# Hybrid decoder trunk on one core: bias table as eight DRAM rows, and one convolution group moved from TensorE to GpSimd

## The chip, the core and the metric

The kernel runs on one NeuronCore of a Trainium2 chip. The metric is the device time of one execution in microseconds (us). Before the change it is 2148.73 us, the median of three runs (2148.67 to 2150.67). Five engines work side by side and meet at semaphores: TensorE (PE; its weight loads are shown as PEld), VectorE (DVE), ScalarE (ACT), GpSimd (POOL) and SyncE (SP), which here only issues DMAs.

## What is computed

One layer of a hybrid decoder over 2064 prompt positions and 8 sample positions. Cut to what matters:

```python
q, k, v, u = project_in(x, norm1_g, w_in)            # rmsnorm, h @ w_in, u = a * sigmoid(b)
s = einsum(q, k) * HEAD_DIM ** -0.5
bias = rel_bias[t5_bucket(clip(dist, 0, WINDOW))]    # table over distance 0..128, one row per head
s = where(valid, s + bias, -inf)                     # then softmax with sinks, and p @ v
c = depthwise_conv(pad(u, 30), conv_w, conv_b)       # causal, 31 taps, 512 channels
c = silu(layernorm(c, conv_ln_g, conv_ln_b))
x = x + concat(attn, c) @ w_out
x = x + relu(rmsnorm(x) @ w_up) ** 2 @ w_down
```

For a query at row p of a block and a key at column j, the bias depends on p - j alone: row p of the table of one head is the row before it shifted by one place.

## The kernel before

Channels lie on the 128 partitions, positions in the free dimension. The positions are cut into five tiles (384, 448, 448, 448 and 320 prompt positions). Every large product is made in three float32r passes: weights and activations are split into a high and a low part, and hi*hi, hi*lo and lo*hi are added in PSUM. One step (`pe_step`) is one slab of 128 output channels: 8 chunks in 3 passes, 24 matmuls, in the order hi, lo of chunk 0, hi, lo of chunk 1 and so on with the weights' high part, then the eight with their low part. ACT and DVE split the next slab meanwhile (`whi`, `wlo`).

Tile 0 goes first. Its input projection has 14 steps: m = 8 to 13 (keys, values, queries), then m = 0 and 1 alone, then m = 2 to 7, each paired with the same slab for tile 1. The steps m = 2c and 2c + 1 give the gate and the values of convolution group c (128 channels), so group 0 is ready after m = 1 and group 3 after m = 7. Then five more steps of tile 1 serve as cover, and the output projection of tile 0 (`wout_step`) reads the attention output (`cah`, `cal`) and the convolution output. From there on the feed-forward part of one tile covers the small work of the next.

Small work comes from generators (`Background`): attention (`attn_gen`), convolution and its layer norm (`conv_gen`), norms. Each step hands out a budget of it in the order of the generators' list, and `sync_bg` writes out what is left. The tile framework then orders every engine's instructions by its own timeline of the program. So the order on an engine isn't the order in the code, and each engine runs its list strictly in order.

Tiles that live long come from `slot()`: one pool of 52 buffers for inputs, normalised chunks, queries, convolution accumulators and scratch. A buffer is handed out again as soon as the program text is done with it, and the first instruction that writes it then waits for the last one that read the tile before it.

The bias: `bias_setup` makes the 8 rows of 384 distances with a small matmul, writes them to DRAM 128 times (`scr`, 1.5 MB, once per partition) and reads them back with a stride one element short of a row, so that each partition gets its shifted row (`bias`). It is called at the sixth input step of tile 0 (BAT = 5). The first score operation of the attention (L562, DVE) needs `bias`.

The convolution of tile 0: DVE runs groups 0 to 2, 31 operations each (one multiply, then 30 multiply-adds over shifted views of u, L122 and L116) into the accumulators `pre[c]`; `conv_pe_gen` runs group 3 on TensorE as 31 matmuls with diagonal weights that ACT builds (`cps`). `misc()` is a single PSUM buffer called `st` that many small products share.

Of the kernel before, what the change touches and what calls it, by code (L numbers as in the profile page):

```python
# [7 lines left out]
F32 = mybir.dt.float32  # L8
F32R = mybir.dt.float32r
AF = mybir.ActivationFunctionType  # L10
ALU = mybir.AluOpType
# [5 lines left out]
NSMP = 8  # L17
HD = 64
NH = 8
WIN = 128  # L20
CW = 31
# [13 lines left out]
EW = 384  # L35
# [3 lines left out]
G1, G2, GF, CWT, CB, LG, LB, SK, SKR = 0, 8, 16, 24, 148, 152, 156, 160, 168  # L39
# [3 lines left out]
STEP = "step"  # L43
# [33 lines left out]
def trunk(tc, x_in, w_all, smalls, rel, ck, cv, sconv, y_out, kv_out, ck_out, cv_out, up_out, us_out):  # L77
    nc = tc.nc
    with ExitStack() as ctx:
# [4 lines left out]
        at = ctx.enter_context(tc.tile_pool(name="at", bufs=1))  # L84
        dr = ctx.enter_context(tc.tile_pool(name="dr", bufs=1, space=bass.MemoryType.DRAM))
# [4 lines left out]
        def ahead(gen, off, cond=None):  # L90
            while True:
                try:
                    if off and (cond is None or cond()):
                        with tc.high_priority(off):
                            r = next(gen)
                    else:
                        r = next(gen)
                except StopIteration:
                    return
                yield r  # L100
# [28 lines left out]
        def act(out, a, f, bias=0.0, scale=1.0, accum_out=None):  # L129
            if accum_out is None:  # L130
                return nc.scalar.activation(out, a, f, bias=bias, scale=scale)  # L131
            return nc.scalar.activation(out, a, f, bias=bias, scale=scale, accum_out=accum_out)  # L132
# [7 lines left out]
        def slot(dt=F32):  # L140
            t = tp.tile([128, TS], dt, tag="t", name="t")
            return t
# [12 lines left out]
        def mm(out, lhsT, rhs, start, stop):  # L155
            return nc.tensor.matmul(out, lhsT, rhs, start=start, stop=stop)  # L156
# [11 lines left out]
        sq0 = cp.tile([128, 1], F32, name="sq0")  # L168
        act(sq0, epst, AF.Sqrt)
        bias = cp.tile([128, NH, 256], F32, name="bias")  # L170
        scr = dr.tile([128, NH, EW], F32, name="scr")

        order = []
        pos = {"dma": 0, "split": 0}
# [532 lines left out]
        def conv_gen(i):  # L707
# [4 lines left out]
            cvs = s["cvs"] = {}  # L712
            pre = [slot() for _ in range(4)] if i == 0 else None
            s["pre"] = pre
            todo = [c for c in range(4) if i > 0 or c not in CPE]
            groups = [todo[j:j + CG] for j in range(0, len(todo), CG)]

            def taps(c, a):
# [102 lines left out]
                tt(s["cvl"][c][:, :r], cvs[c][:, :r], f(s["cvh"][c][:, :r]), ALU.subtract)  # L821
                yield

        def conv_pe_gen(i):
            s = st[i]
            n = RT[i]
            o = OFF[i]
            while "cvs" not in s:
                yield STEP
            dgs = [slot(), slot()]  # L830
            for c in CPE:
                while c not in s.get("udone", []):
                    yield STEP
                u = s["u"][c]
                ps = pm.tile([128, 512], F32, tag="mm", name="cps")
                for k in range(CW):
                    j = CWT + c * CW + k
                    dg = dgs[k // 3 % 2][:, k % 3 * 128:k % 3 * 128 + 128]
                    act(dg, idn, AF.Copy, scale=sm[:, j:j + 1])
                    mm(ps[:, :n], dg, u[:, o + k:o + k + n], k == 0, k == CW - 1)  # L840
                    if k % PEK == PEK - 1:
                        yield STEP
                yield STEP
                a = s["pre"][c]
                act(a[:, :n], ps[:, :n], AF.Identity, bias=sm[:, CB + c:CB + c + 1])
                s["cvs"][c] = a
                yield STEP

# [74 lines left out]
        def bias_setup():  # L923
            ps = misc()
            mm(ps[:NH, :EW], relt[:33, 0:NH], relt[:33, 8:8 + EW], True, True)
            e = slot()
            cpy(e[:NH, :EW], ps[:NH, :EW])
            nc.gpsimd.dma_start(scr.rearrange("p h x -> h p x"),
                                e[:NH, :EW].unsqueeze(1).broadcast_to([NH, 128, EW]))
            a = scr[:]  # L930
            nc.gpsimd.dma_start(bias, bass.AP(tensor=a.tensor, offset=a.offset + 127,
                                              ap=[[NH * EW - 1, 128], [EW, NH], [1, 256]]))

        def ff_budget(i, up):
            t = 24 * (RT[i] / 2400.0 + 0.0025)
# [77 lines left out]
        for op in prog:  # L1013
            k = op[0]
            if k == "in":
                _, i, m = op
                if i == 0:
                    if nin == N1AT:
                        gens["n1"] = [bg.add(g1)]
                    if nin == BAT:  # L1020
                        bias_setup()
                    nin += 1
                win_step(i, m, 24 * (TI[i] / 2400.0) - 1.2 - 0.6)
            elif k == "in2":
                m = op[1]
                win_step(0, m, 24 * (TI[0] / 2400.0) - 1.2 - 0.6, keep=True)
                win_step(1, m, 24 * (TI[1] / 2400.0) - 0.6)
            elif k == "conv0":
                flush()
                gens["conv"] = [bg.add(ahead(conv_gen(0), HP0, lambda: "ln" in st[0])), bg.add(conv_pe_gen(0), True)]  # L1030
            elif k == "attn0":
                flush()
                gens["attn"] = [bg.add(attn_gen(0, range(j, PT[0] // BQ[0], NS0)), A0F) for j in reversed(range(NS0))]
            elif k == "out":
                _, i, m = op
                wout_step(i, m, ff_budget(i, False))
            elif k == "ff":
                _, i, t, g, c = op
                b = ff_budget(i, t == "u")
                if t == "u":  # L1040
                    up_step(i, g * 8 + c, b)
                else:
                    down_step(i, g, c, b)
            elif k == "bg":
                i = op[1]
                flush()
                cat_alloc(i)
                gens["attn"] = [bg.add(attn_gen(i, range(j, PT[i] // BQ[i], NS1))) for j in range(NS1)]
                if i == NT - 1:
                    gens["attn"].append(bg.add(sample_gen(i)))  # L1050
                gens["conv"] = [bg.add(ahead(conv_gen(i), HPC, lambda: "ln" in st[i]))]
            elif k == "sync_bg":
                flush()
                bg.drain(gens["attn"] + gens["conv"])
            elif k == "n1":
                gens["n1"] = [bg.add(norm1_gen(op[1]))]
            elif k == "sync_n1":
                bg.drain(gens["n1"])
            elif k == "n2":
                gens["n2"] = [bg.add(ahead(norm2_gen(op[1]), HPN if op[1] else HPN0))]  # L1060
            elif k == "sync_n2":
                flush()
                bg.drain(gens["n2"])
            elif k == "fin":
                gens["fin"] = [bg.add(ahead(final_gen(op[1]), HPF if op[1] == NT - 1 else 0))]
                if op[1] == NT - 1:
                    flush()
                    bg.drain()
# [16 lines left out]
HPN0 = 300  # L1085
HPF = 0
COV = 5
BAT = 5
N1AT = 3
A0F = False  # L1090
QUICK = ["a0", "a1", "l0", "m0", "b0", "f4"]
NS0 = 2
NS1 = 1
NPB = 2
PEK = 16
CG = 1
PARTS1 = 4
CPE = [3]


def _pack(inp):
# [107 lines left out]
```

## Time and profile before

| | us |
|---|---|
| median of three runs | 2148.73 |
| the profiled execution | 2149.5 |
| its span in the trace | 2147.7 |
| PE busy in the span | 2093.9 (97%) |
| DVE busy in the span | 1524.6 (71%) |
| ACT busy in the span | 1178.0 (55%) |
| POOL busy in the span | 50.2 (2%) |

The profiled execution lies 0.8 us over the median and 1.8 us over its own span. Busy shares are means over the whole span. For a change in one place, read the stretch it lies in: which engine stands idle there, and what ended its idle time. The chain of waits, followed back from the last instruction, tells which engine the end hangs on; the timeline of an engine in a window tells when it stood still and for whom.

### The profile page before, as it was taken

The page shows a single profiled execution, that of the slowest core. Times are in us where ns is not written, and L with a number is a line of the kernel's source. Part 1 is how long each engine was busy: PE and PEld are TensorE (multiplying, and loading weights), DVE is VectorE, ACT ScalarE, POOL GpSimd, SP SyncE. Part 2 cuts the span into 40 slices and gives each one's busy share as a digit, 9 for nine tenths or more (in the row PEclk, how much of TensorE's full clock was granted, in tenths as well). Part 3 has the DMA queues.
Part 4 walks back from the last instruction along what each step waited for, and adds up shares of the span by engine and source line. Part 5 has one row for each costly group of instructions (what it writes and reads, how often), then busy time and mean ns, then how long its engine had stood idle before and what let it go on. Part 6 is the DMA issues. An engine that isn't in the chain of part 4 may idle for free.

```text
span 2147.7 us, 29970 instructions
## 1 busy us (share of the span) xinstructions
PE 2093.9 (97%) x11330; PEld 1963.9 (91%) x11330; DVE 1524.6 (71%) x2595; ACT 1178.0 (55%) x2152; POOL 50.2 (2%) x95
## 2 busy tenths in 40 slices
PE   8599999999999999999999999999999999999998
PEld 7587999999999999999999999999999999999997
DVE  5597598986867988647759887466898754575444
ACT  6357475567546464655445547554655475454443
POOL 1000000000000000000000000000010100000000
PEclk9799999999999999999999999999999999999999
DMA  5411423334443222325432322344433323434443
GB/s 180 79 50 40 138 90 127 118 118 142 156 140 102 98 98 106 101 98 177 139 104 99 105 99 90 107 142 169 144 116 106 124 99 103 151 139 169 148 147 104
DMA packets 77952, 255.67 MB, mean 119 GB/s; under 512 B 9805, under 2 KB 20173, under 8 KB 77808
## 3 DMA queue, kind: packets, MB, share of 16 engines
q1 hardware_dynamic: 72000, 238.08, 32.3%
q0 software_dynamic: 5088, 14.93, 2.5%
q8 instruction: 89, 1.46, 0.3%
q10 hardware_dynamic: 720, 0.76, 0.1%
q14 instruction: 55, 0.45, 0.1%
HBM read 241.97 MB, written 11.75 MB: 118 GB/s over the span
## 4 chain that ended last, share of the span: by engine, by line
PE 94%; issue 2%; DMA 2%; DVE 1%; POOL 0%; ACT 0%; DVEq 0%; POOLq 0%; ACTq 0%
PE mm L156 88%; PE st L156 2%; DMA scr<-t 2%; PE s L156 1%; PE pt L581 1%; PE cps L156 1%; DVE t L116 0%; DMA bias<-scr 0%; DMA t<-x_in 0%; DVE t L112 0%; DVE wlo L112 0%; DVE m L116 0%; PE mx L156 0%; DVE ss L112 0%; PE st L529 0%
## 5 line engine op out<-in xcount | busy, mean ns | idle before, releaser
L156 PE MATMUL mm<-t,whi 128*128 128x448 f32 (+3 forms) x6560 | 1353.2, 352 | 12.8 <-ACT t L131 8.6
L156 PEld LDWEIGHTS mm<-t,whi 128*128 128x128 f32 x6560 | 1170.1, 189 | 84.1 <-ACT t L131 9.5
L135 ACT CAST whi<-raw 128x1024 fp32r<-128x1024 f32 x424 | 443.6, 1049 | 572.8 <-PE mm L156 463.1
L156 PE MATMUL mm<-t,wlo 128*128 128x448 f32 (+3 forms) x3280 | 713.5, 350 | 0.0
L112 DVE TENSOR_TENSOR wlo<-raw,whi 128x1024 fp32r<-128x1024 f32 x424 | 516.8, 1219 | 244.1 <-PE mm L156 125.3
L156 PEld LDWEIGHTS mm<-t,wlo 128*128 128x128 f32 x3280 | 588.8, 188 | 33.6
L116 DVE SCALAR_TENSOR_TENSOR t<-u,sm,t 128x448 f32<-128x448 f32 (+1 forms) x480 | 300.9, 645 | 3.5
L112 DVE TENSOR_TENSOR t<-mm,t 128x448 f32<-128x448 f32 (+2 forms) x200 | 116.6, 583 | 191.5 <-PE mm L156 190.2
L112 DVE TENSOR_TENSOR t<-m,t 128x448 fp32r<-128x448 f32 (+3 forms) x236 | 134.2, 582 | 25.9 <-ACT t L135 25.4
L135 ACT CAST t<-m 128x448 fp32r<-128x448 f32 (+3 forms) x236 | 125.3, 536 | 17.8 <-DVE m L116 13.2
L131 ACT ACTIVATE m<-mm 128x448 f32<-128x448 f32 (+2 forms) x176 | 90.1, 512 | 55.9 <-PE mm L156 50.0
L131 ACT ACTIVATE m<-t 128x448 f32<-128x448 f32 (+3 forms) x140 | 72.0, 543 | 62.1 <-DVE t L112 42.2
L132 ACT ACTIVATE p<-p,nm 112x240 f32<-112x240 f32 (+3 forms) x152 | 72.2, 476 | 50.3 <-DVE nm L121 50.1
L131 ACT ACTIVATE m<-m 128x448 f32<-128x448 f32 (+3 forms) x164 | 90.1, 549 | 3.9
L562 DVE CUSTOM_DVE_ANT_0 p<-s,bias,sm 112x240 f32<-112x240 f32 (+3 forms) x152 | 61.2, 449 | 28.0 <-DMA bias<-scr 25.6
L131 ACT ACTIVATE p<-p,rd 112x240 f32<-112x240 f32 (+3 forms) x152 | 61.9, 476 | 4.7 <-DVE rd L127 4.2
L112 DVE TENSOR_TENSOR ss<-ss,m 128x448 f32<-128x448 f32 (+3 forms) x100 | 58.4, 584 | 6.8 <-ACT m L131 3.3
L116 DVE SCALAR_TENSOR_TENSOR t<-t,sm 128x384 f32<-128x384 f32 (+1 forms) x98 | 57.2, 613 | 2.4 <-ACT t L131 1.9
L127 DVE RECIPROCAL rs<-m 128x448 f32<-128x448 f32 (+2 forms) x15 | 41.6, 2776 | 24.1 <-ACT m L131 24.1
L156 PE MATMUL mm<-cah,whi 128*128 128x448 f32 (+2 forms) x160 | 56.2, 353 | 0.0
L156 PE MATMUL mm<-cal,whi 128*128 128x448 f32 (+2 forms) x160 | 56.0, 352 | 0.0
L920 POOL DMA_DIRECT2D y_out<-t x32 | 17.3, 544 | 1609.6 <-DVE t L116 1607.7
(174 smaller groups left out, 1139.3 us busy)
## 6 DMA issues: line engine op xcount, KB each, us to landing
raw<-w_all SPq DMA_DIRECT2D x424, 512.0 KB, 3.2
t<-x_in SPq DMA_DIRECT2D x40, 224.0 KB, 4.5
y_out<-t POOLq DMA_DIRECT2D x24, 224.0 KB, 3.3
t<-x_in SPq DMA_DIRECT2D x16, 164.0 KB, 3.7
t<-x_in POOLq DMA_DIRECT2D x8, 224.0 KB, 6.5
t<-x_in SPq DMA_DIRECT2D x8, 200.0 KB, 4.7
scr<-t POOLq DMA_DIRECT2D x1, 1536.0 KB, 33.1
t<-x_in SPq DMA_DIRECT2D x8, 192.0 KB, 4.3
```

The costliest lines, as they stand in the source:

```text
L112: return nc.vector.tensor_tensor(out, a, b, op=op)
L116: return nc.vector.scalar_tensor_tensor(out, a, s, b, op0=op0, op1=op1)
L127: return nc.vector.reciprocal(out, a)
L131: return nc.scalar.activation(out, a, f, bias=bias, scale=scale)
L132: return nc.scalar.activation(out, a, f, bias=bias, scale=scale, accum_out=accum_out)
L135: return nc.scalar.copy(out, a)
L156: return nc.tensor.matmul(out, lhsT, rhs, start=start, stop=stop)
L562: nc.vector.tensor_tensor_reduce(out=p[:bq, c, :nk], in0=sp[c // 2][:bq, c % 2, :nk], in1=bias[:bq, h, b0:b0 + nk], scale=1.0, scalar=sm[: ...
L581: nc.tensor.transpose(t[:r, c * bq:(c + 1) * bq], p[:bq, c, a:a + r], idn[:bq, :bq])
L920: q.dma_start(y_out[:, YO[i] + c * n:YO[i] + (c + 1) * n], y[:, :n])
```

## The change

Two edits. First, the bias: `scr` shrinks to 8 copies of the rows (NSMP, which the sample attention still reads), and `bias_setup` moves from the sixth input step to the second (BAT = 1). Two DMAs read overlapping rows from it, so that partition p gets the row shifted by p (`brow`, in the two buffers of the attention's `p`). The shift runs the wrong way round, and four matmuls with an exchange matrix (`flip`, made on POOL) turn the partitions round, each into `st`, from which ACT copies two heads into `bias`. That is called three input steps later. Second, in tile 0 the convolution group on TensorE is dropped; group 0 goes to POOL instead (31 multiplies and 30 adds, with two product buffers), and DVE runs groups 1 to 3.

```diff
-        scr = dr.tile([128, NH, EW], F32, name="scr")
+        scr = dr.tile([NSMP, NH, EW], F32, name="scr")
...
-            todo = [c for c in range(4) if i > 0 or c not in CPE]
+            todo = [c for c in range(4) if i > 0 or c not in CPOOL]
...
-        def conv_pe_gen(i):
+        def conv_pool_gen(i):
...
-            dgs = [slot(), slot()]
-            for c in CPE:
+            prods = [slot(), slot()]
+            for c in CPOOL:
...
-                ps = pm.tile([128, 512], F32, tag="mm", name="cps")
-                for k in range(CW):
-                    j = CWT + c * CW + k
-                    dg = dgs[k // 3 % 2][:, k % 3 * 128:k % 3 * 128 + 128]
-                    act(dg, idn, AF.Copy, scale=sm[:, j:j + 1])
-                    mm(ps[:, :n], dg, u[:, o + k:o + k + n], k == 0, k == CW - 1)
...
-                act(a[:, :n], ps[:, :n], AF.Identity, bias=sm[:, CB + c:CB + c + 1])
+                wc = CWT + c * CW
+                nc.gpsimd.tensor_scalar(a[:, :n], u[:, o:o + n], sm[:, wc:wc + 1], sm[:, CB + c:CB + c + 1],
+                                        op0=ALU.mult, op1=ALU.add)
+                for k in range(1, CW):
+                    p = prods[k % 2]
+                    nc.gpsimd.tensor_scalar(p[:, :n], u[:, o + k:o + k + n], sm[:, wc + k:wc + k + 1], None,
+                                            op0=ALU.mult)
+                    nc.gpsimd.tensor_tensor(a[:, :n], a[:, :n], p[:, :n], op=ALU.add)
...
-                                e[:NH, :EW].unsqueeze(1).broadcast_to([NH, 128, EW]))
+                                e[:NH, :EW].unsqueeze(1).broadcast_to([NH, NSMP, EW]))
             a = scr[:]
-            nc.gpsimd.dma_start(bias, bass.AP(tensor=a.tensor, offset=a.offset + 127,
-                                              ap=[[NH * EW - 1, 128], [EW, NH], [1, 256]]))
+            flip = slot()
+            nc.gpsimd.memset(flip[:, :128], 0.0)
+            nc.gpsimd.affine_select(out=flip[:, :128], in_=flip[:, :128], compare_op=ALU.not_equal, fill=1.0,
+                                    base=-127, pattern=[[1, 128]], channel_multiplier=1)
+            rows = []
+            for j in range(2):
+                t = at.tile([128, 4, 256], F32, tag="p", name="brow", bufs=NPB)
+                nc.gpsimd.dma_start(t, bass.AP(tensor=a.tensor, offset=a.offset + 4 * j * EW,
+                                               ap=[[1, 128], [EW, 4], [1, 256]]))
+                rows.append(t)
+            return flip, rows
+
+        def bias_flip(flip, rows):
+            for h in range(0, NH, 2):
+                ps = misc()
+                mm(ps, flip[:, :128], rows[h // 4][:, h % 4:h % 4 + 2, :], True, True)
+                cpy(bias[:, h:h + 2, :], ps.rearrange("p (h j) -> p h j", h=2))
...
-                        bias_setup()
+                        rows = bias_setup()
+                    if nin == BAT + 3:
+                        bias_flip(*rows)
...
-BAT = 5
+BAT = 1
...
-CPE = [3]
+CPOOL = [0]
```

The framework orders the whole of tile 0 anew. The first place is TensorE after the third step of the queries. `s` are scores, `st` the single buffer, `st<-relt` the eight bias rows, `st<-brow` the flips. Before:

```order
L156 MATMUL mm<-t,whi 128x400 x10
L156 MATMUL mm<-t,wlo 128x400 x8
L156 MATMUL s<-t 128x256 x4
L156 MATMUL st<-m,ones 128x128 x3
L156 MATMUL st<-m,ones 128x64
L156 MATMUL st<-relt 8x384
L156 MATMUL mm<-t,whi 128x400 x16
```

After:

```order
L156 MATMUL mm<-t,wlo 128x400 x3
L156 MATMUL s<-t 128x256 x2
L156 MATMUL st<-brow,t 128x512 x4
L156 MATMUL st<-m,ones 128x128 x3
L156 MATMUL st<-m,ones 128x64
L529 MATMUL st<-idn,t 128x128
L530 MATMUL st<-idn,t 128x128
L156 MATMUL mm<-t,whi 128x400 x16
```

The bias rows' matmul has moved four steps up, and four flips stand in a row in front of the norm's broadcast of tile 1.

The second place is DVE at the start of the convolution of group 1. `t<-m 128x400` is u of a group of tile 0, `L122 ... t<-t,sm` the first operation of a group, `L116 ... t<-t,sm` the others. Before:

```order
L112 TENSOR_TENSOR m<-mm,t 128x400
L116 SCALAR_TENSOR_TENSOR t<-t,sm 128x384
L112 TENSOR_TENSOR t<-m 128x400
L116 SCALAR_TENSOR_TENSOR t<-t,sm 128x384
L122 TENSOR_SCALAR t<-t,sm 128x384
L116 SCALAR_TENSOR_TENSOR t<-t,sm 128x384
```

After, u of group 1 stands 44 rows ahead of these, and u of group 2 another 22 rows behind that:

```order
L112 TENSOR_TENSOR wlo<-raw,whi 128x1024
L112 TENSOR_TENSOR dn<-dn,es 128x4
L122 TENSOR_SCALAR t<-t,sm 128x384 x2
L127 RECIPROCAL rd<-dn 128x4
L112 TENSOR_TENSOR p<-st,p 64x4x128
L116 SCALAR_TENSOR_TENSOR t<-t,sm 128x384 x4
```

Groups 1 and 2 now begin together, well behind their u. In the built program their accumulators take the buffers of two low-part chunks of tile 0's normalised input, and the second product buffer of POOL takes a third; all three wait for matmuls 2, 4 and 6 of step m = 7, the last that reads those chunks. Before, group 0 and 1 had buffers that were free, and group 2 alone waited for m = 7.

The third place is DVE at the end of the convolution. Here `m<-t` and `m<-m,t` add the four groups for the layer norm. Before:

```order
L127 RECIPROCAL rd<-dn 128x4
L112 TENSOR_TENSOR vv<-st,vv 128x128
L112 TENSOR_TENSOR m<-m,t 128x384 x2
L112 TENSOR_TENSOR wlo<-raw,whi 128x1024
L112 TENSOR_TENSOR kk<-mm,kk 64x448 x2
L112 TENSOR_TENSOR p<-st,p 64x4x128
L116 SCALAR_TENSOR_TENSOR t<-mx,t 128x384 x4
```

After:

```order
L112 TENSOR_TENSOR p<-st,p 64x4x128
L116 SCALAR_TENSOR_TENSOR t<-t,sm 128x384 x4
L112 TENSOR_TENSOR cal<-p,cah 64x4x128
L116 SCALAR_TENSOR_TENSOR t<-t,sm 128x384 x43
L112 TENSOR_TENSOR m<-t 128x384
L112 TENSOR_TENSOR m<-m,t 128x384 x2
L116 SCALAR_TENSOR_TENSOR t<-mx,t 128x384 x4
```

The attention of tile 0 is all done by then, and 43 convolution operations stand alone between it and the layer norm.

## Rows read from the trace of the kernel before

**Rows 1.** The page's chain of waits, shares of the span by engine.
```profile
PE 94%; issue 2%; DMA 2%; DVE 1%; POOL 0%; ACT 0%; DVEq 0%; POOLq 0%; ACTq 0%
```

**Rows 2.** Busy time by stretch: stretch and length, engines, granted clock, DMA share.
```profile
75.60:97.40 21.80, 0.03 (x2) 0.01 (x1) 0.95 (x5) 0.00 (x0) 1.50 (x2) 0.59 0.46 93
97.40:152.60 55.20, 55.20 (x287) 51.84 (x288) 53.34 (x120) 30.87 (x74) 0.00 (x0) 0.95 0.14 48
190.80:219.30 28.50, 22.11 (x109) 19.02 (x107) 19.51 (x33) 20.92 (x39) 0.00 (x0) 0.94 0.16 59
252.00:2147.00 1895.00, 1882.94 (x10300) 1776.33 (x10299) 1350.96 (x2245) 1035.22 (x1849) 39.38 (x70) 1.00 0.36 122
```

**Rows 3.** Waits over the span: who waited for whom, us, times, longest.
```profile
POOL bias L931 <- DMA scr<-t: 32.3, 1, 32.3
DVE p L562 <- DMA bias<-scr: 25.6, 1, 25.6
```

**Rows 4.** DMA issues: form, size, median us from issue to landing.
```profile
scr<-t POOLq DMA_DIRECT2D x1, 1536.0 KB, 33.1
bias<-scr POOLq DMA_DIRECT2D x1, 1024.0 KB, 6.0
```

**Rows 5.** Timeline of PE: start us, us, then the instructions, idle before.
```profile
54.42 0.81 PE L156 MATMUL st<-relt 33*8 33x384 f32 x2 [0.62 <-ACT rs L135]
65.32 1.60 PE L156 MATMUL mm<-t,wlo 128*128 128x400 f32 x8
97.40 1.99 PE L156 MATMUL s<-t 128*128 128x144 f32 x8 [21.77 <-DVE mx L562]
100.27 2.87 PE L156 MATMUL mm<-t,wlo 128*128 128x400 f32 x8
140.55 1.07 PE L156 MATMUL mm<-t,whi 128*128 128x400 f32 x5
```

**Rows 6.** The chain of waits in time: the convolution on PE.
```profile
152.81 3.87 PE cps L156 x12
```

**Rows 7.** Timeline of ACT: two copies of 512 columns out of PSUM.
```profile
107.37 1.07 ACT L135 CAST ph<-pt 128x512 fp32r<-128x512 f32 x2 [1.05 <-PE pt L581]
```

**Rows 8.** DVE by form in 97.4:190.8: count, busy us, mean ns, idle.
```profile
L116 DVE SCALAR_TENSOR_TENSOR t<-t,sm 128x384 f32<-128x384 f32 x90 | 52.2, 612 | 0.5
L112 DVE TENSOR_TENSOR wlo<-raw,whi 128x1024 fp32r<-128x1024 f32 x8 | 9.7, 1217 | 0.7 <-issue 0.7
L562 DVE CUSTOM_DVE_ANT_0 p<-s,bias,sm 128x256 f32<-128x256 f32 x14 | 6.0, 477 | 0.0
L112 DVE TENSOR_TENSOR pl<-pt,ph 128x512 fp32r<-128x512 f32 x8 | 5.4, 685 | 0.1
```

**Rows 9.** Timeline of DVE: convolution operations in a row, and the groups' sum.
```profile
112.67 2.21 DVE L116 SCALAR_TENSOR_TENSOR t<-t,sm 128x384 f32<-128x384 f32 x4
190.80 1.14 DVE L112 TENSOR_TENSOR m<-m,t 128x384 f32<-128x384 f32 x2
```

**Rows 10.** Timeline of PE: layer norm and output projection of tile 0.
```profile
205.78 5.05 PE L156 MATMUL mm<-t,whi 128*128 128x448 f32 x16
219.27 0.84 PE L156 MATMUL mm<-t,whi 128*128 128x384 f32 x2 [0.63 <-ACT t L135]
222.79 3.34 PE L156 MATMUL mm<-t,whi 128*128 128x384 f32 x18
```

**Rows 11.** Timeline of POOL: its two sizes of work that read a tile.
```profile
3.42 0.32 POOL masks.py:199 TENSOR_SCALAR_AFFINE_SELECT idn<-idn 128x128 f32<-128x128 f32 x1
3.95 0.19 POOL L653 TENSOR_SCALAR_AFFINE_SELECT dm<-dm 64x8 f32<-64x8 f32 x1
```

**Rows 12.** Timelines of DVE and POOL: the one place with both in a row.
```profile
588.89 4.32 DVE L116 SCALAR_TENSOR_TENSOR t<-t,sm,rs 128x384 f32<-128x384 f32 x8
589.81 4.32 POOL L920 DMA_DIRECT2D y_out<-t x8 [497.94 <-DVE t L116]
```

More of the change, by code (lines that the diff above doesn't have):

```diff
@@ L834, in conv_pe_gen @@
                 u = s["u"][c]
-                ps = pm.tile([128, 512], F32, tag="mm", name="cps")
-                for k in range(CW):
-                    j = CWT + c * CW + k
-                    dg = dgs[k // 3 % 2][:, k % 3 * 128:k % 3 * 128 + 128]
-                    act(dg, idn, AF.Copy, scale=sm[:, j:j + 1])
-                    mm(ps[:, :n], dg, u[:, o + k:o + k + n], k == 0, k == CW - 1)
-                    if k % PEK == PEK - 1:
-                        yield STEP
-                yield STEP
-                a = s["pre"][c]
-                act(a[:, :n], ps[:, :n], AF.Identity, bias=sm[:, CB + c:CB + c + 1])
+                a = s["pre"][c]
+                wc = CWT + c * CW
[6 more added lines that the diff above has]
+                    nc.gpsimd.tensor_tensor(a[:, :n], a[:, :n], p[:, :n], op=ALU.add)
                 s["cvs"][c] = a
@@ L1029, in trunk @@
                 flush()
-                gens["conv"] = [bg.add(ahead(conv_gen(0), HP0, lambda: "ln" in st[0])), bg.add(conv_pe_gen(0), True)]
+                gens["conv"] = [bg.add(ahead(conv_gen(0), HP0, lambda: "ln" in st[0])), bg.add(conv_pool_gen(0), True)]
             elif k == "attn0":
@@ L1094 @@
 NPB = 2
-PEK = 16
 CG = 1
 PARTS1 = 4
-CPE = [3]
+CPOOL = [0]
 def _pack(inp):
```

## The prediction

> **What bounds the kernel now.** I read the chain of waits first: 94% of it is TensorE [rows 1], so a microsecond counts only if TensorE loses or wins it. Then the stretches [rows 2]: from 252 us to the end TensorE is busy for 1882.9 of 1895 us, and the change touches nothing there. It is all about the first 252 us. There the waits [rows 3] show DVE standing 25.6 us for the table, whose read stood 32.3 us behind the write of `scr`, and TensorE's score matmuls standing 21.8 us for DVE [rows 5]. The DMA list agrees: 33.1 us for 1536 KB, then 6.0 us for 1024 KB [rows 4]. The second thing to see is in the stretch behind the hole, 97.4 to 152.6: TensorE is full, but DVE too, at 53.3 of 55.2 us [rows 2]. DVE fills its time with the convolution. The third is the end of tile 0: from 190.8 to 219.3 TensorE is busy 22.1 of 28.5 us, since the output projection waits for the layer norm of the convolution, which ends a chain on DVE. So the hole is followed by a stretch in which two engines are full, and what TensorE saves is kept only if DVE's convolution ends sooner as well.
>
> **What the change removes.** The hole: 21.8 us [rows 5], and with it the restart at a lower clock. After it eight `wlo` matmuls took 2.87 us against 1.60 ahead of it [rows 5], the granted clock of the hole being 0.59 [rows 2]; with the eleven matmuls in front of those eight I count 2.9 us. The convolution on TensorE: 62 records at 3.87 / 12 = 0.32 us [rows 6], 20.0 us, all of it behind 152 us. ACT loses its 31 diagonals, which nobody waited long for.
>
> **The new table.** `scr` is now 96 KB; at the old rate of 1536 KB in 33.1 us that is 2.1 us. The two reads move the old 1024 KB, 6.0 us [rows 4]. The table's matmul was at 54.4 us [rows 5] and stands four steps further up, each 24 matmuls of 0.18 us: near 36 us, so that the reads land near 46 us. The flips stand where that matmul stood, near 53 us: the reads are hidden, with 7 us to spare. The rest of POOL's queue behind them (the sample's bias) has no reader before tile 4. The flips are on the path. 384 columns of such a product cost 0.65 us as a pair of `cps` records [rows 6]; 512 columns cost 0.86 us at that rate. Each must be copied out of the single buffer before the next may start, 0.53 us [rows 7] and a handover of 0.15: four times 1.55 us is 6.2 us of TensorE. It can't cost less than its four products, 3.4 us, as no other matmul stands between them; at the lower clock it is up to 10 us. Behind them tile 1's norm comes later by as much, and DVE has score operations ahead of it that formerly waited: 2 us.
>
> **Where step m = 7 goes.** It began at 140.55 us [rows 5]. Less 21.8 and 2.9, plus 6.2 and 2, it begins at 124, and its sixth matmul frees the last of the three buffers at 125 us.
>
> **What starts then.** That is the step on which I rest the prediction. In the new order DVE runs none of its 93 convolution operations until this point, since the accumulators of groups 1 and 2 take buffers that step m = 7 still reads. POOL stops too: it gets through four of its 61 operations, then waits for its second product buffer, the third of those. Until 125 us DVE has only norms, attention and splits to do, and what it formerly filled in is left for later. From then on it has 93 operations at 0.53 us: one lasts 612 ns [rows 8], and four in a row took 2.21 us [rows 9], so each starts 0.53 us after the one before and overlaps it by 0.08. Together 49 us. Between them the order has 12 score operations of 0.40, 5 splits of 1.14, 14 operations of 512 columns at 0.60 (their means less that overlap [rows 8]) and some 6 us of small ones: 25 us. With 3 us of idle time such as the stretch before had, the groups are added up at 125 + 49 + 25 + 3 = 202 us. Before, that was 191.9 [rows 9].
>
> **From there to the output projection.** Before, 27.3 us lay between that sum and the first matmul on the convolution's output at 219.27 [rows 9, 10]. In the new order less stands between: one step of tile 1 (which takes 5 to 9 us by the clock; its first 16 matmuls took 5.05 us behind a gap [rows 10]) and the attention's 24 matmuls. The bare links add up to 16 us; I take 22. TensorE then has 2.7 us less behind it, as eight attention matmuls that ran up to 222.79 are done already. 202 + 22 - 2.7 = 221.3, against 219.3: **+2 us**, before POOL is counted. So the 45 us that TensorE saves become idle time of TensorE, some 160 to 220 us, waiting for DVE.
>
> **POOL beside DVE.** 57 POOL operations run from 125 us on, in the same time. Their price: 0.19 us for 8 elements, 0.32 for 128 [rows 11], so 1.08 ns an element and 0.57 us for 384; with a second input up to twice the slope, 0.94. That is 32 to 43 us of POOL, so by itself it is done near 165 to 180 us, ahead of DVE. What it does to DVE no row shows: the one place with both in a row has DVE at 4.32 us for eight, its usual 0.54, beside DMA issues [rows 12], but those read no operands. The ends are nothing, and that either engine waits for the other whenever both read their operands. In the second case DVE loses POOL's time except for what POOL does beside DVE operations that read at most one operand from SBUF, about 15 us of the 74: 17 to 28 us. A gain is excluded, as POOL takes no work from DVE: 93 operations before and after. I take exclusion at its middle, +23 us, because the operations have the same form on both engines (long streams over the same tiles, two inputs) and are unlike the DMA issues of rows 12; both ends stay in the range.
>
> The Trainium skill speaks against the change here: the page "SBUF — State Buffer", section "Who interferes with whom", says that a DVE instruction with two SBUF inputs contends with a GpSimd instruction that reads SBUF, under an exclusive lock for the whole instruction. By it the sum would be the upper end, near 28 us; no row of this trace shows it.
>
> **Sum.** 2149.5 (profiled execution) + 2 + 23 = 2174.5 us; less 0.8 us, by which that execution lies over the median, 2173.7, say **2174 us**.
>
> **The rivals.**
> *No contention.* Everything as above with POOL free: 2 us over the median, 2151. For it: [rows 12]. Chance 0.20.
> *TensorE's saving shows.* If DVE isn't late (it would have to find gaps that I count as full, the stretch from the sum to the projection shrinks to 16 us, or POOL and DVE keep out of each other's way while step m = 7 is earlier than 124), the saved 21.8 + 2.9 + 20.0 less 8.2 reach the end in part; all of it would be 36 us, 2112. Half of that is 2130. Against it: 93 operations need 49 us, and they start behind m = 7 in the order. Chance 0.12.
> *POOL is the last (slower).* If a POOL operation takes 1.2 us or more, 57 of them with a DVE operation of 0.53 between take 99 us, to 224; the groups' sum needs group 0, and with what DVE then has left it comes 10 to 20 us later than in my forecast: 2185 to 2195. It decides from about 1.1 us an operation on. Chance 0.10.
> *The table isn't there in time.* If the new DMAs take as long as the old (33.1 + 6.0 us from 36 us on), the flips wait till 75 us, and TensorE stands 22 us in front of them: 2196. Chance 0.05.
> My forecast keeps 0.53.
>
> **Chances and range.** A difference of 0.2% (4.3 us) is about what a measurement of this kernel can tell. Faster: the second rival and a sliver of the first, 0.14. Within 0.2%: two thirds of the first and the low edge of the forecast, 0.15. Slower: 0.71. The range takes in the forecast with exclusion at both ends (2168 to 2180, and 6 us more for the 22 us and the start at 125), no contention below it and POOL as the last above: 2145 to 2192.
>
> **What would show it.** The changed profile should have no wait of DVE for the table, and four flips with ACT copies between them near 53 to 60 us. Step m = 7 should start near 124 us. DVE should run no convolution before that, then be full till 200 to 230 us, and TensorE should have gaps there that add up to over 40 us, ended by DVE. POOL should stop after its fourth operation for a matmul. Contention would show as convolution operations on DVE longer than 0.61 us while POOL works, and at 0.61 again when it has ended. If they stay at 0.61, the 23 us fall; if the groups' sum comes before 190 us, the whole forecast falls.

## The result and the profile after

The changed kernel takes 2177.7 us (median of four runs, 2176.5 to 2179.0) against 2148.7: a ratio of 1.0133, 95% interval 1.0115 to 1.0151. It is slower by 1.3%, some 29 us. The profiled execution took 2176.5 us, with a span of 2174.6, against 2149.5 and 2147.7 before.

The two bias edits did what they were to do. These are the changed kernel's waits over the span, in the columns of [rows 3]; the two waits shown there are gone, and two others have come:

```profile
PE mx L156 <- DVE m L112: 39.3, 1, 39.3
POOL t L841 <- PE mm L156: 41.9, 1, 41.9
```

TensorE stands 39.3 us for `m`, the sum of the four convolution groups, ahead of the layer norm's statistics (`mx`). GpSimd stands 41.9 us for a matmul, in the middle of its convolution. In the chain of waits by engine, to be read against [rows 1], DVE's share has gone from 1% to 5%, and what stood on DMA and on nothing (issue) has shrunk:

```profile
PE 93%; DVE 5%; ACT 1%; DMA 1%; issue 0%; SPq 0%; DVEq 0%; ACTq 0%
```

By stretch, in the columns of [rows 2]: the old hole and the stretch from 160 to 252 us, both of after, and under them the second of before:

```profile
75.60:97.40 21.80, 21.64 (x118) 20.63 (x119) 10.38 (x29) 14.69 (x38) 4.15 (x4) 1.00 0.15 49
160.00:252.00 92.00, 26.37 (x94) 20.83 (x93) 79.14 (x115) 25.39 (x51) 47.48 (x37) 0.59 0.12 40
```
```profile
160.00:252.00 92.00, 85.61 (x414) 73.31 (x414) 64.03 (x123) 57.58 (x120) 0.00 (x0) 0.96 0.25 86
```

The hole is filled: 21.6 of 21.8 us busy, where [rows 2] had 0.03. But from 160 to 252 us TensorE is busy for 26.4 us in place of 85.6, and DVE and GpSimd (the third and fifth numbers) are what runs. TensorE's timeline has the five marks by which the prediction can be followed: a flip behind its wait, the slow restart behind the flips (granted clock 0.53 from 62 to 68 us, mostly the lower of its two levels, 1.2 GHz), step m = 7, the statistics, and the first matmul on the convolution's output.

```profile
53.05 1.13 PE L156 MATMUL st<-brow,t 128*128 128x512 f32 x2 [0.68 <-ACT bias L135]
62.17 5.67 PE L156 MATMUL mm<-t,whi 128*128 128x400 f32 x16 [1.36 <-DVE m L112]
125.47 0.34 PE L156 MATMUL mm<-t,whi 128*128 128x400 f32 x1
227.42 1.65 PE L156 MATMUL mx<-m,ones 128*128 128x384 f32 x2 [39.34 <-DVE m L112]
248.01 2.31 PE L156 MATMUL mm<-t,whi 128*128 128x384 f32 x6 [2.19 <-ACT t L135]
```

The last stood at 219.27 [rows 10]. It is 28.7 us later, and the span is 26.9 us longer.

DVE's timeline shows its first convolution operation, the last 43, and the groups' sum ([rows 9] has the sum of before):

```profile
126.94 1.33 DVE L122 TENSOR_SCALAR t<-t,sm 128x384 f32<-128x384 f32 x2
197.59 28.13 DVE L116 SCALAR_TENSOR_TENSOR t<-t,sm 128x384 f32<-128x384 f32 x43
226.22 1.15 DVE L112 TENSOR_TENSOR m<-m,t 128x384 f32<-128x384 f32 x2
```

GpSimd's timeline shows its first three operations, the one behind its wait, and the last:

```profile
80.08 0.66 POOL L837 TENSOR_SCALAR t<-t,sm 128x384 f32<-128x384 f32 x1 [41.55 <-ACT m L131]
80.72 1.25 POOL L841 TENSOR_SCALAR t<-t,sm 128x384 f32<-128x384 f32 x1
82.05 1.01 POOL L843 TENSOR_TENSOR t<-t 128x384 f32<-128x384 f32 x1
...
126.31 1.75 POOL L841 TENSOR_SCALAR t<-t,sm 128x384 f32<-128x384 f32 x1 [41.90 <-PE mm L156]
...
207.23 1.04 POOL L843 TENSOR_TENSOR t<-t 128x384 f32<-128x384 f32 x1
```

DVE by form from 60 to 250 us (columns as in [rows 8]) is the view that shows the contention. The first three forms read their tile operands from SBUF, the last two take one from PSUM (`pt`, `s`):

```profile
L116 DVE SCALAR_TENSOR_TENSOR t<-t,sm 128x384 f32<-128x384 f32 x90 | 69.4, 824 | 0.4
L112 DVE TENSOR_TENSOR wlo<-raw,whi 128x1024 fp32r<-128x1024 f32 x12 | 16.6, 1386 | 6.5 <-ACT p L132 2.6 <-PE mm L156 2.4 <-ACT whi L135 1.3
L122 DVE TENSOR_SCALAR t<-t,sm 128x384 f32<-128x384 f32 x3 | 2.5, 868 | 0.0
L112 DVE TENSOR_TENSOR pl<-pt,ph 128x512 fp32r<-128x512 f32 x10 | 6.6, 680 | 7.1 <-ACT ph L135 7.1
L562 DVE CUSTOM_DVE_ANT_0 p<-s,bias,sm 128x256 f32<-128x256 f32 x14 | 6.0, 477 | 0.1
```

A tap (one of the 90 multiply-adds) lasts 824 ns in place of 612 [rows 8], the split `wlo` 1386 in place of 1217; `pl` and `p` keep their 685 and 477 (676 and 481 in the stretch 152 to 180 us, with GpSimd at work all the time). The same form in two stretches, 180 to 208.3 us with GpSimd at work and 208.3 to 225.6 us after its end:

```profile
L116 DVE SCALAR_TENSOR_TENSOR t<-t,sm 128x384 f32<-128x384 f32 x27 | 24.9, 987 | 0.1
```
```profile
L116 DVE SCALAR_TENSOR_TENSOR t<-t,sm 128x384 f32<-128x384 f32 x32 | 18.2, 630 | 0.2
```

With GpSimd a tap takes 987 ns; as soon as GpSimd has ended, 630. Yet the two engines don't shut each other out for the whole length of an operation: the 28.3 us from 180 to 208.3 hold 11 products and 11 sums of GpSimd, 24.9 us at the 1.25 and 1.01 us that they take alone, and 27 taps of DVE, 14.3 us at 0.53 each. Even if one of each is cut by the edges, that is over 36 us of work in 28.

### The profile page after: what moved, and what is told of

It reads as the page before. It is cut to its first block, busy times and chain, and to the rows that moved or that the text cites. A ratio compares the mean times of both kernels' runs of the same rounds, so it can differ in the third digit from the quotient of the medians.

```text
span 2174.6 us, 29903 instructions
## 1 busy us (share of the span) xinstructions
PE 2080.6 (96%) x11276; PEld 1953.9 (90%) x11276; DVE 1549.2 (71%) x2595; ACT 1172.1 (54%) x2126; POOL 135.8 (6%) x159
## 4 chain that ended last, share of the span: by engine, by line
PE 93%; DVE 5%; ACT 1%; DMA 1%; issue 0%; SPq 0%; DVEq 0%; ACTq 0%
PE mm L156 88%; DVE t L116 4%; PE st L156 2%; PE s L156 1%; PE pt L581 1%; DMA raw<-w_all 0%; DVE wlo L112 0%; DMA sm<-smalls 0%; DVE p L562 0%; DVE m L116 0%; DVE m L112 0%; DVE t L112 0%; DVE pl L112 0%; PE mx L156 0%; DVE cal L112 0%
## 5 line engine op out<-in xcount | busy, mean ns | idle before, releaser
L116 DVE SCALAR_TENSOR_TENSOR t<-u,sm,t 128x448 f32<-128x448 f32 (+1 forms) x480 | 300.8, 645 | 3.5
L116 DVE SCALAR_TENSOR_TENSOR t<-t,sm 128x384 f32<-128x384 f32 (+1 forms) x98 | 74.3, 808 | 2.5 <-ACT t L131 2.1
```

The source lines that it names most:

```text
L116: return nc.vector.scalar_tensor_tensor(out, a, s, b, op0=op0, op1=op1)
```

## The experiments

Two causes are to be told apart, which the prediction had added up: the **late start** (three buffers that step m = 7 frees) and the **contention** of GpSimd and DVE. The rivals are that only one of them counts, that the bias edit costs something itself, and that the output projection waits for something else. Ratios are to the kernel before, with 95% intervals. Where an edit is long, the line shown stands for the whole of it.

### Each edit by itself

The bias edit alone (`scr`, `bias_setup`, `bias_flip` and BAT as changed; the convolution of before):

```diff
-CPOOL = [0]
+CPE = [3]
```

> The bias edit alone; the convolution stays as before (group 3 on TensorE, groups 0 to 2 on DVE). Theory: the new table is a gain and the moved convolution is what costs. TensorE loses the hole (21.8 us) and the restart behind it (2.9), and gets four flips (about 7 us as the changed kernel's trace shows them). Groups 0 and 1 have buffers of their own again, so DVE works on them before step m = 7 begins. About 17 us fewer than before: 2130 to 2137. Rival: the early table, not the convolution, is what costs (score work that comes earlier pushes DVE's convolution back, so that the output projection waits as in the changed kernel): 2149 or more.

2129.6 us, ratio 0.9909 (0.9894 to 0.9924): 20 us faster, 0.4 us under the expected range. Groups 0 and 1 begin at 81 and 91 us, ahead of step m = 7, with no wait for a buffer. TensorE doesn't wait for the groups' sum; of the waits at the statistics the one for the squares is left, 3.5 us as before the change:

```profile
81.09 0.48 DVE L122 TENSOR_SCALAR t<-t,sm 128x384 f32<-128x384 f32 x1
90.83 0.47 DVE L122 TENSOR_SCALAR t<-t,sm 128x384 f32<-128x384 f32 x1
```
```profile
187.88 0.83 PE L156 MATMUL mx<-ones,ss 128*128 128x1 f32 x6 [3.45 <-DVE ss L112]
```

The convolution edit alone (table as before):

```diff
-BAT = 1
+BAT = 5
```

> The convolution edit alone: the bias table as before, group 0 on GpSimd, groups 1 to 3 on DVE. The accumulators of groups 1 and 2 and GpSimd's second product buffer wait here for score matmuls, which stand behind the hole of some 22 us. Theory: the moved group costs by itself what contention makes of DVE's taps, about 20 us, and the 20 us that TensorE saves are not seen: 2165 to 2190, slower than before. Rival: the moved group is a gain or nothing by itself and costs only together with the new table: 2130 to 2152.

2192.7 us, ratio 1.0194 (1.0180 to 1.0207), 2.7 us over the expected range. By itself the moved group costs 42 us, and the two edits add up to less (20 off, 42 on: 22) than the 29 measured. The gap, 0.30% in the ratios, is little more than the half widths of the three intervals allow together (0.27%), and where it comes from wasn't traced. I had taken the score matmuls that free the buffers to come soon after the hole. They come late: GpSimd goes on at 143 us, and DVE begins its groups at 144, 17 us later than with both edits.

```profile
143.23 1.25 POOL L841 TENSOR_SCALAR t<-t,sm 128x384 f32<-128x384 f32 x1 [46.36 <-PE s L156]
```

### The late start and the contention, one at a time

More buffers, so that nothing waits for step m = 7:

```diff
-NSLOT = 52
+NSLOT = 55
```

> The changed kernel with 55 buffers in the pool of slots in place of 52, so that no convolution accumulator and no product buffer has to wait for step m = 7. The work is the same and GpSimd still runs group 0 beside DVE. Theory of two causes (late start and contention, each about 20 us of the wait in front of the layer norm's statistics): the taps start before 126 us, the groups' sum comes near 205 in place of 227, and the time is about 2155. Rival, contention alone: DVE was full anyway and loses as much to GpSimd wherever the taps stand, 2172 to 2180. Rival, late start alone: the whole wait of 39 us goes, 2135 to 2140.

2151.0 us, ratio 1.0007 (0.9998 to 1.0017): 27 us of the 29 are gone, with the contention still there (taps at 765 ns). The groups' sum ends at 203.0 us in place of 227.4, and TensorE's wait there is 6.7 us:

```profile
L116 DVE SCALAR_TENSOR_TENSOR t<-t,sm 128x384 f32<-128x384 f32 x90 | 66.9, 765 | 0.8
```
```profile
203.08 1.65 PE L156 MATMUL mx<-m,ones 128*128 128x384 f32 x2 [6.74 <-DVE m L112]
```

GpSimd short, with the late start kept:

```diff
-                    nc.gpsimd.tensor_scalar(p[:, :n], u[:, o + k:o + k + n], sm[:, wc + k:wc + k + 1], None,
+                    nc.gpsimd.tensor_scalar(p[:, :8], u[:, o + k:o + k + 8], sm[:, wc + k:wc + k + 1], None,
                                             op0=ALU.mult)
-                    nc.gpsimd.tensor_tensor(a[:, :n], a[:, :n], p[:, :n], op=ALU.add)
+                    nc.gpsimd.tensor_tensor(a[:, :8], a[:, :8], p[:, :8], op=ALU.add)
```

> The changed kernel with GpSimd's 30 products and 30 sums of group 0 on 8 columns in place of 384; the taps 1 to 30 of that group are left out of the other columns. Buffers, waits and DVE's own work stay. Theory of two causes: a DVE tap lasts 0.61 us again in place of 0.82, the groups' sum comes some 20 us sooner, near 205 to 208, and the time is about 2155. Rival, no contention (a tap is longer for a reason that lies on DVE, or the sum waits for GpSimd's end): the taps stay at 0.82 us and the time at 2177, or the taps stay long and the time falls.

2154.9 us, ratio 1.0021 (1.0012 to 1.0031). Taps are back at 609 ns and the sum ends at 204.7 us:

```profile
L116 DVE SCALAR_TENSOR_TENSOR t<-t,sm 128x384 f32<-128x384 f32 x90 | 49.8, 609 | 0.3
```
```profile
204.71 1.65 PE L156 MATMUL mx<-m,ones 128*128 128x384 f32 x2 [30.58 <-DVE m L112]
```

This is the prediction's sum without the contention, measured: 204.7, where it said 202. It also shows who loses now. An 8-column product takes 0.31 us where DVE is idle; beside DVE two of them took 4.92 us, while DVE's operations of that stretch kept their lengths (`pl` 0.64 us, a tap 0.6, `wlo` 1.20):

```profile
81.64 0.31 POOL L841 TENSOR_SCALAR t<-t,sm 128x8 f32<-128x8 f32 x1
...
139.57 4.92 POOL L841 TENSOR_SCALAR t<-t,sm 128x8 f32<-128x8 f32 x2
```

Both at once:

> Both at once: 55 buffers, and GpSimd's products and sums of group 0 on 8 columns (the taps 1 to 30 of that group are left out of the other columns). Theory of two causes that add up: taps start before step m = 7 and last 0.61 us, the groups' sum comes near 185 and TensorE's wait in front of the statistics is gone: 2130 to 2137. Rival, a third cause behind these two (the output projection waits for something else, such as attention or ACT): 2145 or more.

2138.3 us, ratio 0.9948 (0.9933 to 0.9963). The buffers take 1.26% off the changed kernel's ratio, the short operations 1.12%, both together 1.85%: they overlap by a fifth of their sum. The result lies 1.3 us over the expected range: the sum ends at 189.9 us, five later than I had put it, and TensorE still waits 7.4 us for it. The third-cause rival would have been 2145 or more. That doesn't make the two causes the whole of it: the version set beside this one under "A better version" shows a third part.

### What the group is worth on each engine

All four groups on DVE, with 55 buffers:

```diff
-CPOOL = [0]
+CPOOL = []
```

> The changed kernel with 55 buffers and all four groups of tile 0 on DVE; GpSimd has no convolution, TensorE neither. DVE has 31 operations of 0.53 us more, 16.4 us, and no neighbour. Theory: with GpSimd beside it DVE lost about as much as these 31 operations take, so this is within 5 us of the 55-buffer version with GpSimd (2151): 2148 to 2156. Rival 1, GpSimd takes more off DVE than it costs: 2158 or more. Rival 2, GpSimd costs more than it takes off: 2146 or less.

2147.0 us, ratio 0.9986 (0.9977 to 0.9995), 1 us under the expected range, 1 us over rival 2, and below the 1.0007 (0.9998 to 1.0017) of the version with GpSimd. DVE does 31 operations more, and its sum ends at 199.4 us, where GpSimd's help had it at 203.0.

```profile
L116 DVE SCALAR_TENSOR_TENSOR t<-t,sm 128x384 f32<-128x384 f32 x120 | 68.5, 609 | 0.6
```

120 taps without a neighbour keep DVE busy for 68.5 us; 90 taps beside GpSimd took 66.9. With the first operations of the groups (1.9 and 2.8 us) it is 70.4 against 69.7: GpSimd cost DVE about as much as it took from it. The 3.6 us by which the sum differs come for the most part from the start: from 80 to 92 us DVE is busy for 10.3 us with group 0 to work on, and for 7.4 us where GpSimd has that group and DVE's first tap must wait for group 1. The Trainium skill, page "Perfetto Trace Analysis", section "Optimizing Scalar/DVE Operations", says that moving operations between VectorE and GpSimd might not help, since they share a read port; here it doesn't.

### What holds what up

GpSimd's product in another form:

```diff
-                    nc.gpsimd.tensor_scalar(p[:, :n], u[:, o + k:o + k + n], sm[:, wc + k:wc + k + 1], None,
-                                            op0=ALU.mult)
+                    nc.gpsimd.tensor_scalar(p[:, :n], u[:, o + k:o + k + n], sm[:, wc + k:wc + k + 1], zc,
+                                            op0=ALU.mult, op1=ALU.add)
```

`zc` is a column of zeros, made at the start.

> The changed kernel with GpSimd's 30 products written as multiply and add of a column of zeros in place of a bare multiply. The one operation of this form in the changed kernel takes 0.66 us where the bare multiplies beside it take 1.25. If the form is what makes the bare multiply slow, the 30 products take about 20 us in place of 46, GpSimd ends 20 us earlier, holds DVE up for less, and the time falls to 2162 to 2172. Rival: the first operation is short for another reason (nothing runs beside it): products stay at 1.25 us or more and the time at 2175 to 2180.

2169.9 us, ratio 1.0093 (1.0079 to 1.0107). The time is in the range, but one step on the way to it failed. Alone, the two-operation form takes 0.66 us, as expected. Beside DVE the 30 products take 1575 ns on average, no less than the 1553 of the bare form, and GpSimd ends 83 us after step m = 7 as before. What became shorter is DVE's loss: 767 ns a tap in place of 824, 90 x 57 ns = 5.1 of the 7.8 us. So GpSimd's span didn't follow the length of its product, and DVE's loss did.

```profile
84.28 0.66 POOL L843 TENSOR_SCALAR t<-t,sm,zc 128x384 f32<-128x384 f32 x1
```
```profile
L843 POOL TENSOR_SCALAR t<-t,sm,zc 128x384 f32<-128x384 f32 x30 | 47.1, 1575 | 43.3 <-PE mm L156 43.2
L116 DVE SCALAR_TENSOR_TENSOR t<-t,sm 128x384 f32<-128x384 f32 x90 | 64.2, 767 | 0.3
```

Then writing against reading. The first try replaced the products and sums by 60 fills:

> The changed kernel with GpSimd's 30 products and 30 sums replaced by 60 fills of 384 columns with zero: GpSimd writes into the same buffers and reads none (the taps 1 to 30 of group 0 are left out). The order on DVE is another one here, so only the length of DVE's taps while GpSimd fills is compared, not the time. Theory, the engines exclude each other when both read operands: taps stay at 0.61 us. Rival, writing is enough to hold DVE up: taps above 0.65 us in the stretch of the fills.

This tells nothing of DVE. With no product to wait for, the fills (0.42 us each) ran from 83 to 107.6 us, and DVE's taps came behind 106: they hardly met. One run, 2145.6 us. The second try kept the 8-column operations, so that the waits and DVE's order stayed, and put a fill ahead of each product and one behind each sum:

```diff
+                    nc.gpsimd.memset(p[:, :n], 0.0)
                     nc.gpsimd.tensor_scalar(p[:, :8], u[:, o + k:o + k + 8], sm[:, wc + k:wc + k + 1], None,
                                             op0=ALU.mult)
                     nc.gpsimd.tensor_tensor(a[:, :8], a[:, :8], p[:, :8], op=ALU.add)
+                    nc.gpsimd.memset(p[:, :n], 0.0)
```

> The version with GpSimd's operations on 8 columns, with two fills of 384 columns added to each of the 30 products' buffers, 60 in all of some 0.42 us: 25 us of writing beside DVE's taps, and DVE's order is the same as without them (the taps 1 to 30 of group 0 are still left out of the other columns). If reading is what holds DVE up, its taps stay at 0.61 us and the time at 2152 to 2158. If writing holds DVE up too, DVE loses up to those 25 us: taps near 0.8 us and 2165 to 2180.

2154.0 us, ratio 1.0021 (1.0011 to 1.0030), the same as without the fills. 25 us of writing, nearly all of it from 126.5 to 177 us, where DVE has 44 of its 90 taps (614 ns on average), cost DVE nothing:

```profile
L845 POOL MEMSET t<- 128x384 f32 x30 | 12.7, 422 | 0.2
```
```profile
L116 DVE SCALAR_TENSOR_TENSOR t<-t,sm 128x384 f32<-128x384 f32 x90 | 50.1, 612 | 0.3
```

This and the forms of after (two operands from SBUF longer, one from PSUM not) agree with the Trainium skill, page "SBUF — State Buffer", section "Who interferes with whom": a DVE instruction with two SBUF inputs contends with a GpSimd instruction that reads SBUF, and not with one that only writes. It also names `tensor_scalar` among those that can contend; the first operation of a group (475 ns before, 868 now) did. The exclusive lock for the whole instruction, which the prediction took from the same section, isn't borne out by the lengths in the profile: over 36 us of the two engines' work were done in 28.

### A better version

The bias edit with more buffers, and then with the flips in the steps' three rotating buffers, two input steps later in the program:

```diff
-NSLOT = 52
+NSLOT = 55
```

> The bias edit alone with 55 buffers, the flips in st as in the changed kernel. It parts the 12.9 us that the version with 55 buffers and rotated flips (2116.7) has over the bias edit alone (2129.6). Theory: it is the flips. In the bias edit alone TensorE is full from 77 us to the layer norm, so earlier taps give it nothing but the 3.5 us in front of the norm's statistics: 2125 to 2130. Rival: it is the buffers, and 2116 to 2121.

2124.5 us, ratio 0.9883 (0.9867 to 0.9900), half a microsecond under the range: 5 us for the buffers, a little more than the 3.5 I saw in front of the statistics, and the rest of the 12.9 for the flips.

This version also shows what the two causes leave over. Beside it stands the changed kernel with both causes taken off (2138.3 us). Both have 55 buffers, the flips in `st`, and 90 taps on DVE of 610 and 608 ns. Yet the statistics start 16 us later there, and the time is 13.8 us longer, though TensorE is spared the 20 us of its group:

```profile
173.97 0.81 PE L156 MATMUL mx<-m,ones 128*128 128x384 f32 x2
```
```profile
189.95 1.65 PE L156 MATMUL mx<-m,ones 128*128 128x384 f32 x2 [7.39 <-DVE m L112]
```

The groups' sum ends at 170.6 and at 189.9 us. From 80 us to there DVE is busy for 84.9 of 90.6 and for 99.6 of 109.9 us: some 13 us more of other work (attention and splits) stands ahead of the sum, and DVE idles 4.6 us more. Its first tap comes at 80.7 and at 91.5 us, since group 0, the first to be ready, isn't DVE's any more. So the new order and the choice of the group have a share beside the two causes. No run moves another group, and these two aren't parted.

```diff
-                ps = misc()
+                ps = misc(True)
                 mm(ps, flip[:, :128], rows[h // 4][:, h % 4:h % 4 + 2, :], True, True)
...
-                    if nin == BAT + 3:
+                    if nin == BAT + 5:
                         bias_flip(*rows)
```

> The bias edit alone (group 3 on TensorE again), with 55 buffers, and the flips written one input step after the last of the queries and into the three rotating buffers of the steps (mx) in place of the single st. They stand between other matmuls then, and none waits for the copy of the one before. Expected against the bias edit alone (2129.6): the three waits of 0.68 us, the norm's broadcast that stood behind them and a part of the slow restart at 63 us go, 3 to 7 us: 2122 to 2127. Rival: the flips were no longer on the path that sets the end, since DVE or the layer norm is late there: 2128 to 2132.

2116.7 us, ratio 0.9845 (0.9832 to 0.9858): 1.5% faster than before and 2.8% faster than the changed kernel, and 5 us under the expected range. The flips gave 8 us more, where 3 to 7 had been expected of them and the buffers together. In the stretch 30 to 75 us (bias edit with 55 buffers, then this version) TensorE is busy for 3.9 us more, and the granted clock has no dip:

```profile
30.00:75.00 45.00, 40.31 (x199) 35.51 (x198) 31.95 (x58) 27.55 (x57) 2.73 (x4) 0.92 0.38 121
```
```profile
30.00:75.00 45.00, 44.19 (x239) 40.00 (x237) 39.95 (x83) 33.11 (x67) 2.73 (x4) 1.00 0.39 120
```

The sixteen matmuls behind the flips, 5.7 us at the lower clock in the first (granted 0.50 from 62 to 68 us), are 3.31 us here (granted 1.00):

```profile
53.79 3.31 PE L156 MATMUL mm<-t,whi 128*128 128x400 f32 x16
```

Last, the changed convolution with all of that:

```diff
-CPE = [3]
+CPOOL = [0]
```

> The changed kernel, group 0 on GpSimd, with 55 buffers and the flips in the rotating buffers one step after the queries: all that made 2116.7 of the bias edit, and only the convolution is another. Theory: the convolution on DVE and GpSimd is the bound here, so TensorE's gain at the flips (8 us there) shows only as far as it lets step m = 1 and the taps begin sooner: 2140 to 2150. Rival: the flips' gain shows in full and the moved group costs no more than TensorE's 20 us: 2128 to 2138.

2144.6 us, ratio 0.9978 (0.9968 to 0.9988), inside the expected range. One group on GpSimd in place of TensorE costs 28 us even in the best surroundings I found, though TensorE is spared 20 us of work. The groups' sum ends at 193.8 us here and at 164.2 in the version with TensorE.

## Why the prediction was right, step by step

The prediction was 2174 us; 2177.7 was measured, inside the range. Its time axis held within 3 us at each mark but the last:

| Mark | predicted | measured |
|---|---|---|
| first flip on TensorE, near | 53 | 51.4 |
| four flips up to the norm's broadcast | 6.2 us | 7.1 us |
| step m = 7 | 124 | 125.5 |
| DVE's first tap behind it | 125 | 126.9 |
| groups' sum without the contention | 202 | 204.7 |
| what GpSimd adds to it | 23 us | 22.7 us |
| groups' sum | 225 | 227.4 |
| from there to the output projection | 22 us | 20.6 us |
| work that TensorE has less behind it | 2.7 us | 1.8 us |
| end of GpSimd | 165 to 180 | 208.3 |

**The table and the hole.** Right. These are the DMA issues of after, in the columns of [rows 4]:

```profile
scr<-t POOLq DMA_DIRECT2D x1, 96.0 KB, 3.7
brow<-scr POOLq DMA_DIRECT2D x2, 512.0 KB, 7.0
```

`scr` took 3.7 us (estimated 2.1), the reads 7.0 (estimated 6.0), and they were in time. The flips cost a little more than was summed. The restart at the lower clock behind them (5.67 us for sixteen matmuls, 4.45 in the kernel before) wasn't in the sum; the version with rotating flips shows that it was worth removing.

**The late start.** Right, and the larger of the two causes: three more buffers take 27 us off, short GpSimd operations 23. It was read from the order and from who reads which buffer.

**From step m = 7 to the sum.** Right: 77 us were forecast from the point where the buffers come free; with GpSimd short it is 127.2, where GpSimd goes on, to 204.7, 77.5 us.

**The contention.** That the engines hold each other up was right, and it was a choice between two ends that no row could decide. That the size came out, 23 against 22.7, is luck: two terms in it were off and cancelled. GpSimd's price: 0.57 and 0.94 us were estimated from its affine selects [rows 11] (their slope of 1.08 ns an element gives 0.60 and 1.01), and alone it takes 1.25 for the bare product and 1.01 for the sum. What DVE loses of that: I let it lose all of GpSimd's time but 15 us. By form DVE lost 17.2 us on the taps (69.4 less 52.2), 2.0 on the splits (12 x 0.169), 1.2 on the first operations and about 1 on small ones, 21.5 in all, over 57 GpSimd operations: 0.38 us each, a third of GpSimd's own time. The rest GpSimd waits itself: it needed 82 us from 126.3 to 208.3, 1.44 us an operation. Had I known the price and kept the rule, the contention would have been some 49 us (57 x 1.13 less 15), and the forecast 26 us higher, at 2200.

**GpSimd as the last.** The rival's own condition was met (1.44 us an operation, over 1.1), and it still didn't come: GpSimd ended 17 us ahead of DVE. Its working put a DVE operation of 0.53 between every two of GpSimd's on top of their price. A measured operation already holds that wait. GpSimd would have been last from (225.6 - 126.3) / 57 = 1.74 us an operation, waits included.

**TensorE's saving.** The 45 us did become idle time, in one wait of 39.3 us and several of the attention. TensorE's idle time over the span grew from 53.8 to 94.0 us. That the rival's 2130 is nearly what the bias edit gives without the moved group (2129.6) is chance: that version keeps the group on TensorE.

## What to carry to other kernels

Before work is taken from the engine that is busy for 97%, find the engine that the next join waits for: here DVE, and the moved group slowed just that one. GpSimd isn't a free engine beside a DVE that streams two SBUF operands; here DVE lost a third of the time that GpSimd's operations take alone, so count such a loss in, and give it work that only writes or that runs while DVE reads PSUM. A change of order that seems to cost nothing can move an accumulator into a buffer that is freed late, so read which tile each new buffer held, and try a few more buffers first. A group moved to one engine also changes which groups the others run: ask what the busiest of them has to do until its new first group is ready.

## What the runs showed of the hardware

A bare product on GpSimd, 384 columns by a scalar of each partition, took 1.25 us, while a product with an added scalar took 0.66 in the same place (from start to start 1.33 and 0.75): adding an operation made it nearly twice as fast. Why isn't shown.

The contention goes both ways, and in these runs it hit the short operation hardest: GpSimd's 8-column product, 0.31 us alone, averaged 0.73 us over 30, of which 28 ran beside DVE, while DVE's taps kept their 0.61. With 384 columns on both sides DVE's tap went from 0.61 to 0.99, and GpSimd's pair of product and sum from 2.26 to 2.65 us (1469 and 1182 ns in the stretch 180 to 208.3 us).

Writing alone, 60 fills of 0.42 us, left DVE's taps beside them at 0.61 us.
